# Weight buffers and branch outputs moved to other start addresses modulo 512 bytes, in a hybrid attention block

## The chip, the cores and the metric

The kernel runs on one core of a Trainium2 chip. The metric is device time in microseconds for one execution. Matmuls run on TensorE (PE in the profile, its weight loads PEld), elementwise work on VectorE (DVE), ScalarE (ACT) and GpSimd (POOL); SyncE (SP) issues most DMAs.

## What is computed

One layer of a hybrid decoder trunk, for a sequence of 256 rows of 2048 float32 values. Cut to what matters:

```python
proj = x @ w_in                       # 2048 -> 15632 columns, split into 14 parts
ya = gla(aq, ak, av, alr) * silu(agate)
yb = sliding_window(bq, bk, bv, sinks) * silu(bgate)
yc = moba(cq, ck, cv) * silu(cgate)   # 256 rows are one block: causal attention
up = einsum('bsnw,nwd->bsnd', stack([ya, yb, yc]), w_branch)
merged = sum(sigmoid(mgate + b_merge) * up, over the 3 branches)
out = merged @ w_o
return layer_norm(2 ** 0.25 * x + out)
```

Nearly all of the work is in the four groups of dense products: x with w_in, the three branch outputs with w_branch, and the merged stream with w_o.

## The kernel before, in words

**Precision.** Every float32 operand of a dense product is split into a high part (rounded to the format fp32r) and a low part (the rest, in fp32r too). A product is three fp32r matmuls: high with high, low with high, high with low.

**Weights.** `seq` lists all weight chunks in the order in which they are used. `emit_chunk` (line 112) handles one: SyncE loads it into a raw buffer (tag `wraw`, 4 buffers), ACT copies it to the high part (line 136, tag `whi`, 3 buffers), DVE subtracts to get the low part (line 137, tag `wlo`, 3 buffers). High and low buffers turn round together, so chunk i uses buffer i modulo 3 of both. `next_chunk` keeps two chunks ahead of the one in use. A chunk is 512 rows by 256 (or 260) columns, or 256 rows by 512 columns.

**Two forms of dense product.** In `mm3` (line 237) the weights are stationary and the activations move. For each block of 128 rows and each 128 columns there is a pair: line 242 has the high weights stationary and 512 moving columns (high and low part of the activation side by side), line 244 has the low weights stationary and 256 moving columns (the high part). `proj` calls it with `xhl` as moving operand, `up_mm` with a branch output (`ya`, `yb`, `yc`). There are 2080 such pairs, 384 of them with a branch output. In `nmm` (line 280) the activations are stationary and the weights move: lines 284, 285 and 286 have high, low and again high weights moving, 512, 260 or 256 columns at a time; the stationary operand is `xhl` or `mhl`, and that of line 284 is loaded again for line 285. There are 160 such triples of 512 columns (cv and the first three column groups of w_o), 128 of 260 columns (av), 32 of 256 columns (the fourth group of w_o, wo3 below) and 32 of 256 columns for the last group (wo4), whose weights lie in `wlasth` and `wlastl`, two buffers of the tag `y`.

**Order on TensorE.** While the dense products run, `tick` puts in steps of the attention jobs after each chunk; these are small matmuls between the pairs. Each matmul comes with a weight load of its own stationary operand, which the profile shows as PEld and which starts while the matmul before is running.

**Where the buffers begin.** Buffers are given out in the order of the pools, one behind another, each rounded up to 32 bytes; inside a pool, in the order of first use. Only the start modulo 512 bytes changes here. Before: all three low buffers begin at 160 and all three high buffers at 352, because 1152 columns are 4608 bytes, nine times 512, and the pool `stat` (3 times 64 bytes) stands between them. `xhl` and `mhl` (tag `x`) begin at 416, and so do both buffers of the tag `y`, which hold in turn `xst` (the raw x at the start), `ya`, `yb`, `yc`, `wlasth` and `wlastl`. A 128-column stationary operand is 512 bytes in a partition, and every step over rows or columns is a multiple of 512 bytes (except in av, whose rows are 260 columns), so each operand keeps its buffer's start modulo 512.

Of the kernel before, what the change touches and what calls it, by code (L numbers as in the profile page):

```python
# [9 lines left out]
F32 = mybir.dt.float32  # L10
F32R = mybir.dt.float32r
# [6 lines left out]
P = 128  # L18
S = 256
D = 2048  # L20
KT = D // P
# [7 lines left out]
NV = 260  # L29
KC = 4  # L30
RCOLS = KC * NV + 8
WCOLS = 1152
NWARM = 8


# [1 line left out]
def kernel(ctx: ExitStack, tc: tile.TileContext, xT: bass.AP, x: bass.AP, w_in: bass.AP,  # L37
                             w_up: bass.AP, gla_b: bass.AP, norm_g: bass.AP, sinks: bass.AP, b_merge: bass.AP,
                             w_branch: bass.AP, w_o: bass.AP, ln_g: bass.AP, ln_b: bass.AP, out: bass.AP):
    nc = tc.nc  # L40

    const = ctx.enter_context(tc.tile_pool(name="const", bufs=1))
    wraw = ctx.enter_context(tc.tile_pool(name="wraw", bufs=4))
    wlo = ctx.enter_context(tc.tile_pool(name="wlo", bufs=3))


    stat = ctx.enter_context(tc.tile_pool(name="stat", bufs=3))
    whi = ctx.enter_context(tc.tile_pool(name="whi", bufs=3))
    mvp = ctx.enter_context(tc.tile_pool(name="mvp", bufs=2))
    acts = ctx.enter_context(tc.tile_pool(name="acts", bufs=1))  # L50
    work = ctx.enter_context(tc.tile_pool(name="work", bufs=2))
    pp = ctx.enter_context(tc.tile_pool(name="pp", bufs=2, space=PSUM))
    pa = ctx.enter_context(tc.tile_pool(name="pa", bufs=4, space=PSUM))


    seq = []

    def deep(cols):
        return 2 if cols == 512 else KC

    def plan(src, rows, col0, cols, name):
        kc = deep(cols)
        for h in range(rows // (kc * P)):
            seq.append((src, h * kc * P, col0, cols, f"{name}_{h}"))
# [33 lines left out]
    for g, (c0, cols) in enumerate(OUT_COLS):  # L98
        plan(w_o, D, c0, cols, f"wo{g}")

    AHEAD = 2
    ready = []
    state = {"out": 0, "in": 0}
    last = {}

    def load_x(k0, k1):
        xs = xst[:, k0:k1, :]
        nc.sync.dma_start(xs, xT[:, k0:k1, :])
        nc.scalar.copy(xhl[:, k0:k1, 0:S], xs)
        nc.vector.tensor_tensor(xhl[:, k0:k1, S:2 * S], xs, xhl[:, k0:k1, 0:S].bitcast(F32), op=ALU.subtract)  # L110

    def emit_chunk():
        i = state["in"]
        state["in"] += 1
        src, row0, col0, cols, name = seq[i]
        kc = deep(cols)

        def shaped(t):
            return t.rearrange("p (k c) -> p k c", c=cols)
        raw = shaped(wraw.tile([P, RCOLS], F32, tag="wraw", name=f"w{name}")[:, :kc * cols])  # L120
        if name.startswith("wo4_"):
            if not last:
                last["h"] = acts.tile([P, KT, 256], F32R, tag="y", name="wlasth", bufs=2)
                last["l"] = acts.tile([P, KT, 256], F32R, tag="y", name="wlastl", bufs=2)
            k0 = KC * int(name[4:])
            hi, lo = last["h"][:, k0:k0 + KC, :], last["l"][:, k0:k0 + KC, :]
        else:
            hi = shaped(whi.tile([P, WCOLS], F32R, tag="whi", name=f"h{name}")[:, :kc * cols])
            lo = shaped(wlo.tile([P, WCOLS], F32R, tag="wlo", name=f"l{name}")[:, :kc * cols])
        view = src[row0:row0 + kc * P, col0:col0 + cols].rearrange("(k p) c -> p k c", p=P)  # L130
        cuts = [0, 1, 2] if i < 2 else [0, kc]
        for a, b in zip(cuts, cuts[1:]):
            if name.startswith("aq_"):
                load_x(row0 // P + a, row0 // P + b)
            nc.sync.dma_start(raw[:, a:b, :], view[:, a:b, :])
            nc.scalar.copy(hi[:, a:b, :], raw[:, a:b, :])  # L136
            nc.vector.tensor_tensor(lo[:, a:b, :], raw[:, a:b, :], hi[:, a:b, :].bitcast(F32), op=ALU.subtract)  # L137
        ready.append((name, hi, lo))

    def next_chunk(name):  # L140
        while state["in"] < len(seq) and state["in"] <= state["out"] + AHEAD:
            emit_chunk()
        got, hi, lo = ready[state["out"]]
        assert got == name, (got, name)
        state["out"] += 1
        return hi, lo
# [14 lines left out]
        while jobs:  # L161
            tick()

    xhl = acts.tile([P, KT, 2 * S], F32R, tag="x", name="xhl")
    xst = acts.tile([P, KT, S], F32, tag="y", name="xst", bufs=2)


    wz = const.tile([P, 512], mybir.dt.bfloat16, name="wz")
# [134 lines left out]
    def to_y(y, kt, o, gate, name):  # L303
        t = work.tile([P, S], F32, tag="q1", name=f"ty{name}", bufs=4)
        nc.vector.scalar_tensor_tensor(t, o, 0.5, gate, op0=ALU.mult, op1=ALU.mult)
        nc.scalar.copy(y[:, kt, 0:S], t)
        nc.gpsimd.tensor_tensor(y[:, kt, S:2 * S], t, y[:, kt, 0:S].bitcast(F32), op=ALU.subtract)
# [6 lines left out]
    for k in range(0, KT, 2):  # L314
        hi, lo = next_chunk(f"aq_{k // 2}")
# [8 lines left out]
        nc.scalar.copy(av[:, :, NV * g:NV * (g + 1)], ps[:, :, 0:NV])  # L324
    agate = act_tile("agate")

    ya = acts.tile([P, 8, 2 * S], F32R, tag="y", name="ya", bufs=2)
    aq = aqk[:, 0:4, :]
    ak = aqk[:, 4:8, :]
    IT = 1.0 / 16.0  # L330
# [168 lines left out]
    def front_job():  # L499
        yield from gla_job()  # L500
        while not done:
            yield 1
        yield from keys_job()
        yield from in_turn(swa_job, 8, 6)
# [31 lines left out]
                nc.scalar.copy(ks[rows, g, 0, :], src)  # L536
                nc.vector.tensor_tensor(ks[rows, g, 1, :], src, ks[rows, g, 0, :].bitcast(F32), op=ALU.subtract)

    yb = acts.tile([P, 8, 2 * S], F32R, tag="y", name="yb", bufs=2)

    def swa_job(hp):

# [10 lines left out]
        nc.gpsimd.dma_start(qs[0:64, 1, :], ql[64:128, :])  # L553
        yield from wait(4)
        sm = work.tile([P, 2, 2, P], F32, tag="sm", name=f"smb{hp}", bufs=2)
        st = stat.tile([P, 12], F32, tag="st", name=f"stb{hp}")
        nm, den, es = (st[:, 4 * i:4 * i + 4].rearrange("p (j t) -> p j t", j=2) for i in range(3))
        for j in range(2):
            ps = pa.tile([P, 4, P], F32, tag="pa", name=f"sb{hp}{j}")
# [120 lines left out]
    for g in range(4):  # L680
        gate_to(cgate[:, 2 * g:2 * g + 2, :], f"cg{g}")

    yc = acts.tile([P, 8, 2 * S], F32R, tag="y", name="yc", bufs=2)

    def moba_job(hp):
        scale = 128.0 ** -0.5
        sm = work.tile([P, 2, 3 * P], F32, tag="sm", name=f"smc{hp}", bufs=2)
        st = stat.tile([P, 12], F32, tag="st", name=f"stc{hp}")
        nm, den = (st[:, 4 * i:4 * i + 4].rearrange("p (t j) -> p t j", t=2) for i in range(2))
        for j in range(2):  # L690
            h = 2 * hp + j
            ps = pa.tile([P, 512], F32, tag="pa", name=f"sc{hp}{j}")
            nc.tensor.matmul(ps[:, 0:P], cq[:, h, 0:P], ck[:, h, 0:P], start=True, stop=True)
            nc.tensor.matmul(ps[:, P:3 * P], cq[:, h, P:S], ck[:, h, :], start=True, stop=True)
            nc.vector.scalar_tensor_tensor(sm[:, j, :], ps[:, 0:3 * P], scale,
                                           mska.rearrange("p a b -> p (a b)"), op0=ALU.mult, op1=ALU.add)
        parts = (slice(0, P), slice(P, 3 * P))
        for t in range(2):
            nc.vector.tensor_reduce(nm[:, t, :], sm[:, :, parts[t]], axis=AX.X, op=ALU.max, negate=True)
        for j in range(2):  # L700
            for t in range(2):
                nc.scalar.activation(sm[:, j, parts[t]], sm[:, j, parts[t]], AF.Exp, bias=nm[:, t, j:j + 1],
                                     accum_out=den[:, t, j:j + 1])
        nc.vector.reciprocal(den, den)
        for j in range(2):
            for t in range(2):
                nc.vector.tensor_scalar(sm[:, j, parts[t]], sm[:, j, parts[t]], den[:, t, j:j + 1], None,
                                        op0=ALU.mult)
        yield 1
        yield 1  # L710
        yield 1
        ptb = work.tile([P, 2, 3 * P], F32, tag="ptb", name=f"ptbc{hp}", bufs=1)
        for j in range(2):
            pt = pa.tile([P, 512], F32, tag="pa", name=f"ptc{hp}{j}")
            for b in range(3):
                nc.tensor.transpose(pt[:, b * P:(b + 1) * P], sm[:, j, b * P:(b + 1) * P], ident)
            nc.scalar.copy(ptb[:, j, :], pt[:, 0:3 * P])
        yield 1
        po = pa.tile([P, 2, S], F32, tag="pa", name=f"oc{hp}")
        for j in range(2):  # L720
            vs = slice((2 * hp + j) * P, (2 * hp + j + 1) * P)
            nc.tensor.matmul(po[:, j, :], cv[:, 0, vs], ptb[:, j, 0:S], start=True, stop=False,
                             skip_group_check=True)
            nc.tensor.matmul(po[:, j, P:S], cv[:, 1, vs], ptb[:, j, S:3 * P], start=False, stop=True,
                             skip_group_check=True)
        for j in range(2):
            h = 2 * hp + j
            to_y(yc, h, po[:, j, :], cgate[:, h, :], f"c{h}")

    jobs.append(in_turn(moba_job, 4, 4))  # L730
    merge(1, yb)
    drain()
    merge(2, yc)

    mhl = acts.tile([P, KT, 2 * S], F32R, tag="x", name="mhl")
    for dg in range(8):
        ks = slice(2 * dg, 2 * dg + 2)
        nc.scalar.activation(mhl[:, ks, 0:S], merged[dg], AF.Copy, scale=0.5)
# [90 lines left out]
```

## Time and profile before

| what | value |
|---|---|
| median of 3 runs | 965.49 us (964.96 to 965.79) |
| the profiled execution | 964.69 us |
| its span, first to last instruction | 963.0 us |
| PE busy | 946.2 us, 98% of the span, 5598 matmuls |
| PEld, DVE, ACT, POOL busy | 833.9, 633.7, 500.3, 93.0 us |
| mean granted TensorE clock | 0.995 |

Of the rows of the page and the trace: a matmul's duration covers its way through a pipeline, so durations of successive matmuls overlap; how fast they follow one another is read from their starts. In the timeline the columns are the start in us, the duration in us, the engine, the line, the operation, output and inputs by name, the shape and the count. In groups by line they are the line, engine, operation, names, shape and count, then the busy time in us of the group (overlaps counted once) and the mean duration in ns of one, then idle time before. Where a group's matmuls are longer than the distance from each to the next but one of another line, its busy time is that of the whole stage.

### The profile page before, as it was taken

What the parts mean: (1) busy time and instruction counts of PE and PEld (TensorE: products, weight loads), DVE (VectorE), ACT (ScalarE), POOL (GpSimd) and SP (SyncE); (2) the same over time, 40 slices, a digit from 0 to 9 for tenths busy, and PEclk for the clock granted to TensorE, in tenths of its full rate; (3) what the DMA queues carried; (4) which work ended last, traced back from release to release, by engine and by line L of the source; (5) the groups of instructions that cost most, each with busy time, mean ns of one, the idle gap of its engine ahead of it and who ended that gap; (6) DMA issues with size and microseconds to landing.
All of it is one profiled execution on the core that took longest, in us unless ns stands there. A gap on an engine that the chain in (4) does not pass through costs nothing.

```text
span 963.0 us, 14360 instructions
## 1 busy us (share of the span) xinstructions
PE 946.2 (98%) x5598; PEld 833.9 (87%) x5598; DVE 633.7 (66%) x780; ACT 500.3 (52%) x735; POOL 93.0 (10%) x127
## 2 busy tenths in 40 slices
PE   8999999999999999999999999999999999999995
PEld 6899889998888888888888888888888888888885
DVE  6544698758878888865544456665656565685556
ACT  6444564457566666644444445654545454564341
POOL 8000000003112322310000000110000000000003
PEclk9999999999999999999999999999999999999998
DMA  9766665555766666676766666487666666655652
GB/s 309 202 194 183 181 174 170 152 137 155 208 180 183 184 169 192 175 221 196 197 188 185 196 190 183 131 263 220 196 197 192 190 191 194 196 185 190 191 177 88
DMA packets 164052, 180.64 MB, mean 188 GB/s; under 512 B 6048, under 2 KB 150336, under 8 KB 163472
## 3 DMA queue, kind: packets, MB, share of 16 engines
q1 hardware_dynamic: 161552, 174.02, 62.5%
q0 software_dynamic: 2144, 5.51, 1.8%
q8 instruction: 44, 0.72, 0.3%
q10 hardware_dynamic: 288, 0.20, 0.1%
q14 instruction: 24, 0.20, 0.1%
HBM read 176.43 MB, written 2.10 MB: 185 GB/s over the span
## 4 chain that ended last, share of the span: by engine, by line
PE 93%; DVE 4%; DMA 1%; issue 1%; ACT 1%; SPq 0%; POOL 0%; DVEq 0%
PE psmg L242 18%; PE psmg L244 9%; PE pu L242 9%; PE pu L244 4%; PE psbq L242 3%; PE psag L242 3%; PE pscq L242 3%; PE pscg L242 3%; PE psck L242 3%; PE pswo L285 3%; PE pswo L284 3%; PE pswo L286 3%; PE psav L284 2%; PE psav L285 2%; PE psav L286 2%; PE pscv L285 2%
## 5 line engine op out<-in xcount | busy, mean ns | idle before, releaser
L242 PE MATMUL psmg<-xhl,hmg 128*128 128x512 f32 x768 | 264.6, 391 | 0.0
L244 PE MATMUL psmg<-xhl,lmg 128*128 128x256 f32 x768 | 212.1, 276 | 0.0
L137 DVE TENSOR_TENSOR lmg<-wmg,hmg 128x1024 fp32r<-128x1024 f32 x96 | 120.2, 1252 | 75.1 <-ACT hmg L136 75.1
L242 PEld LDWEIGHTS psmg<-xhl,hmg 128*128 128x128 f32 x768 | 144.2, 188 | 29.2
L136 ACT CAST hmg<-wmg 128x1024 fp32r<-128x1024 f32 x96 | 100.6, 1048 | 100.4 <-PE psmg L242 34.1
L244 PEld LDWEIGHTS psmg<-xhl,lmg 128*128 128x128 f32 x768 | 144.2, 188 | 0.1
L137 DVE TENSOR_TENSOR lwb<-wwb,hwb 128x1024 fp32r<-128x1024 f32 x48 | 58.8, 1225 | 38.7 <-ACT hwb L136 38.6
L136 ACT CAST hwb<-wwb 128x1024 fp32r<-128x1024 f32 x48 | 50.3, 1047 | 50.8 <-PE psmg L242 46.9
L137 DVE TENSOR_TENSOR lwo<-wwo,hwo 128x1024 fp32r<-128x1024 f32 x28 | 34.2, 1222 | 27.9 <-ACT hwo L136 27.9
L136 ACT CAST hwo<-wwo 128x1024 fp32r<-128x1024 f32 x28 | 29.4, 1050 | 42.0 <-PE pswo L286 38.9
L285 PE MATMUL pswo<-lwo,mhl 128*128 128x512 f32 (+1 forms) x128 | 47.3, 369 | 0.0
L284 PE MATMUL pswo<-hwo,mhl 128*128 128x512 f32 (+1 forms) x128 | 47.2, 368 | 0.0
L286 PE MATMUL pswo<-hwo,mhl 128*128 128x512 f32 (+1 forms) x128 | 46.6, 364 | 0.0
L242 PE MATMUL psbq<-xhl,hbq 128*128 128x512 f32 x128 | 45.6, 399 | 0.0
L242 PE MATMUL psbg<-xhl,hbg 128*128 128x512 f32 x128 | 44.7, 393 | 0.0
L242 PE MATMUL psag<-xhl,hag 128*128 128x512 f32 x128 | 44.6, 393 | 0.0
L242 PE MATMUL pu<-yb,hwb 128*128 128x512 f32 x128 | 44.2, 391 | 0.0
L242 PE MATMUL pu<-ya,hwb 128*128 128x512 f32 x128 | 44.2, 390 | 0.0
L242 PE MATMUL pu<-yc,hwb 128*128 128x512 f32 x128 | 43.9, 389 | 0.0
L242 PE MATMUL pscq<-xhl,hcq 128*128 128x512 f32 x128 | 43.6, 389 | 0.0
L242 PE MATMUL pscg<-xhl,hcg 128*128 128x512 f32 x128 | 43.6, 389 | 0.0
L242 PE MATMUL psck<-xhl,hck 128*128 128x512 f32 x128 | 43.6, 389 | 0.0
(309 smaller groups left out, 2343.7 us busy)
## 6 DMA issues: line engine op xcount, KB each, us to landing
wmg<-in_w_in_dram SPq DMA_DIRECT2D x96, 512.0 KB, 3.7
wwb<-in_w_branch_dram SPq DMA_DIRECT2D x48, 512.0 KB, 3.5
wwo<-in_w_o_dram SPq DMA_DIRECT2D x32, 512.0 KB, 4.6
wav<-in_w_in_dram SPq DMA_DIRECT2D x16, 520.0 KB, 3.7
wag<-in_w_in_dram SPq DMA_DIRECT2D x16, 512.0 KB, 3.9
wbq<-in_w_in_dram SPq DMA_DIRECT2D x16, 512.0 KB, 3.7
wbg<-in_w_in_dram SPq DMA_DIRECT2D x16, 512.0 KB, 3.7
wcq<-in_w_in_dram SPq DMA_DIRECT2D x16, 512.0 KB, 3.7
```

Of the source, the lines that this page charges most:

```text
L136: nc.scalar.copy(hi[:, a:b, :], raw[:, a:b, :])
L137: nc.vector.tensor_tensor(lo[:, a:b, :], raw[:, a:b, :], hi[:, a:b, :].bitcast(F32), op=ALU.subtract)
L242: nc.tensor.matmul(ps, hi[:, k, c], rhs[:, k0 + k, :], start=first and k == 0, stop=False, skip_group_check=True)
L244: nc.tensor.matmul(ps[:, 0:S], lo[:, k, c], rhs[:, k0 + k, 0:S], start=False, stop=last and k == kc - 1, skip_group_check=True)
L284: nc.tensor.matmul(ps[:, t, :cols], sh, hi[:, k, :], start=kk == 0, stop=False, skip_group_check=True)
L285: nc.tensor.matmul(ps[:, t, :cols], sh, lo[:, k, :], start=False, stop=False, skip_group_check=True)
L286: nc.tensor.matmul(ps[:, t, :cols], sl, hi[:, k, :], start=False, stop=kk == KT - 1, skip_group_check=True)
```

## The change

The widths of the high and low buffers differ and are no longer multiples of 512 bytes, so each of the three buffers begins elsewhere; two small pads (64 bytes each, written once by GpSimd) and the pool `mvp` (64 bytes) stand around them; the pool `stat` goes, and its tile becomes a tag of `work` with three buffers as before; the tiles of the tags `x` and `y` get 48 and 32 more columns. After it, modulo 512, the low buffers begin at 224, 288 and 352 (buffers 0, 1, 2), the high buffers at 480, 96 and 224; `xhl` and `mhl` stay at 416; the `y` buffers begin at 96 (`xst`, `yb`, `wlasth`) and 224 (`ya`, `yc`, `wlastl`). No instruction but the two memsets is added or removed, and no loop changes.

```diff
-WCOLS = 1152
+LCOLS = 1040
+HCOLS = 1056
...
+    pad0 = ctx.enter_context(tc.tile_pool(name="pad0", bufs=1))
     wlo = ctx.enter_context(tc.tile_pool(name="wlo", bufs=3))
-    stat = ctx.enter_context(tc.tile_pool(name="stat", bufs=3))
+    mvp = ctx.enter_context(tc.tile_pool(name="mvp", bufs=2))
     whi = ctx.enter_context(tc.tile_pool(name="whi", bufs=3))
-    mvp = ctx.enter_context(tc.tile_pool(name="mvp", bufs=2))
+    pad1 = ctx.enter_context(tc.tile_pool(name="pad1", bufs=1))
...
+    for pool in (pad0, pad1):
+        nc.gpsimd.memset(pool.tile([P, 16], F32, tag="pad", name=f"pad{pool is pad1:d}"), 0.0)
...
+    def y_tile(dt, name):
+        return acts.tile([P, KT * S + 32], dt, tag="y", name=name, bufs=2)[:, 0:KT * S]
...
-                last["h"] = acts.tile([P, KT, 256], F32R, tag="y", name="wlasth", bufs=2)
-                last["l"] = acts.tile([P, KT, 256], F32R, tag="y", name="wlastl", bufs=2)
+                last["h"] = y_tile(F32R, "wlasth").rearrange("p (k c) -> p k c", k=KT)
+                last["l"] = y_tile(F32R, "wlastl").rearrange("p (k c) -> p k c", k=KT)
...
-            hi = shaped(whi.tile([P, WCOLS], F32R, tag="whi", name=f"h{name}")[:, :kc * cols])
-            lo = shaped(wlo.tile([P, WCOLS], F32R, tag="wlo", name=f"l{name}")[:, :kc * cols])
+            hi = shaped(whi.tile([P, HCOLS], F32R, tag="whi", name=f"h{name}")[:, :kc * cols])
+            lo = shaped(wlo.tile([P, LCOLS], F32R, tag="wlo", name=f"l{name}")[:, :kc * cols])
...
-    xhl = acts.tile([P, KT, 2 * S], F32R, tag="x", name="xhl")
-    xst = acts.tile([P, KT, S], F32, tag="y", name="xst", bufs=2)
+    xhl = acts.tile([P, KT * 2 * S + 48], F32R, tag="x", name="xhl")[:, 0:KT * 2 * S].rearrange("p (k c) -> p k c", k=KT)
+    xst = y_tile(F32, "xst").rearrange("p (k c) -> p k c", k=KT)
...
-    ya = acts.tile([P, 8, 2 * S], F32R, tag="y", name="ya", bufs=2)
+    ya = y_tile(F32R, "ya").rearrange("p (k c) -> p k c", k=8)
...
-        st = stat.tile([P, 12], F32, tag="st", name=f"stb{hp}")
+        st = work.tile([P, 12], F32, tag="st", name=f"stb{hp}", bufs=3)
```

(`yb`, `yc`, `mhl` and the second `st` change in the same way as `ya`, `xhl` and the first `st`.)

## Rows read from the trace of the kernel before

**Rows 1.** The page: span, PE and PEld busy, and the chain by engine.

```profile
span 963.0 us, 14360 instructions
...
PE 946.2 (98%) x5598; PEld 833.9 (87%) x5598; DVE 633.7 (66%) x780; ACT 500.3 (52%) x735; POOL 93.0 (10%) x127
...
PE 93%; DVE 4%; DMA 1%; issue 1%; ACT 1%; SPq 0%; POOL 0%; DVEq 0%
```

**Rows 2.** Waits of PE: who it waited for, total us, times, longest.

```profile
PE psbg L244 <- DVE lbg L137: 1.5, 2, 1.3
```

**Rows 3.** Timeline of PE in ck: one pair and the next.

```profile
470.26 0.39 PE L242 MATMUL psck<-xhl,hck 128*128 128x512 f32 x1
470.49 0.28 PE L244 MATMUL psck<-xhl,lck 128*128 128x256 f32 x1
470.60 0.39 PE L242 MATMUL psck<-xhl,hck 128*128 128x512 f32 x1
```

**Rows 4.** Groups of PE by line and shape: the line 242 of four stages.

```profile
L242 PE MATMUL psmg<-xhl,hmg 128*128 128x512 f32 x768 | 264.6, 391 | 0.0
L242 PE MATMUL psbq<-xhl,hbq 128*128 128x512 f32 x128 | 45.6, 399 | 0.0
...
L242 PE MATMUL psag<-xhl,hag 128*128 128x512 f32 x128 | 44.6, 393 | 0.0
...
L242 PE MATMUL psck<-xhl,hck 128*128 128x512 f32 x128 | 43.6, 389 | 0.0
```

**Rows 5.** Timeline of PE in bq: a pair, and four pairs after its start.

```profile
177.98 0.40 PE L242 MATMUL psbq<-xhl,hbq 128*128 128x512 f32 x1
178.21 0.28 PE L244 MATMUL psbq<-xhl,lbq 128*128 128x256 f32 x1
...
179.38 0.40 PE L242 MATMUL psbq<-xhl,hbq 128*128 128x512 f32 x1
```

**Rows 6.** Timeline of PE in w_o, 512 columns: line 284, 13 triples apart.

```profile
900.15 0.40 PE L284 MATMUL pswo<-hwo,mhl 128*128 128x512 f32 x1
...
909.30 0.40 PE L284 MATMUL pswo<-hwo,mhl 128*128 128x512 f32 x1
```

**Rows 7.** Timeline of PE in av, 260 columns: line 284, 8 triples apart.

```profile
87.75 0.28 PE L284 MATMUL psav<-hav,xhl 128*128 128x260 f32 x1
...
90.62 0.28 PE L284 MATMUL psav<-hav,xhl 128*128 128x260 f32 x1
```

**Rows 8.** Timeline of PE in wo3, 256 columns: line 284, 11 triples apart.

```profile
932.17 0.28 PE L284 MATMUL pswo<-hwo,mhl 128*128 128x256 f32 x1
...
936.06 0.28 PE L284 MATMUL pswo<-hwo,mhl 128*128 128x256 f32 x1
```

**Rows 9.** Timeline of PE in wo4, weights in the y buffers: line 284, 14 triples apart.

```profile
940.66 0.28 PE L284 MATMUL pswo<-wlasth,mhl 128*128 128x256 f32 x1
...
945.69 0.28 PE L284 MATMUL pswo<-wlasth,mhl 128*128 128x256 f32 x1
```

**Rows 10.** Windows: length, busy us (count) of PE, PEld, DVE, ACT, POOL, clock, DMA share.

```profile
464.00:506.00 42.00, 42.00 (x235) 36.56 (x234) 21.62 (x20) 17.68 (x19) 0.00 (x0) 1.00 0.70 198
178.00:179.60 1.60, 1.60 (x11) 1.39 (x10) 1.46 (x2) 1.16 (x3) 0.00 (x0) 1.00 0.90 266
900.00:910.00 10.00, 10.00 (x45) 8.00 (x43) 6.19 (x8) 4.20 (x4) 0.00 (x0) 1.00 0.56 172
...
940.00:944.00 4.00, 4.00 (x35) 4.00 (x35) 2.10 (x5) 0.81 (x1) 0.00 (x0) 1.00 0.00 0
```

**Rows 11.** Timeline of PE and POOL: two attention matmuls, POOL's last set-up, its first user.

```profile
288.39 0.40 PE L596 MATMUL ob<-ph,vz 128*64 128x512 f32 x1
288.63 0.28 PE L598 MATMUL ob<-pl,vz 128*128 128x256 f32 x1
...
16.97 0.25 POOL L369 MEMSET alr<- 128x192 f32 x1
...
25.95 0.56 POOL L235 CAST lmask<-lmf 128x448 int32<-128x448 f32 x1
...
106.67 0.62 PE L354 MATMUL pdd<-hld,ones 128*128 128x512 f32 x2
```

More of the change, by code (lines that the diff above doesn't have):

```diff
@@ L537, in keys_job @@
                 nc.vector.tensor_tensor(ks[rows, g, 1, :], src, ks[rows, g, 0, :].bitcast(F32), op=ALU.subtract)
-    yb = acts.tile([P, 8, 2 * S], F32R, tag="y", name="yb", bufs=2)
+    yb = y_tile(F32R, "yb").rearrange("p (k c) -> p k c", k=8)
     def swa_job(hp):
@@ L681 @@
         gate_to(cgate[:, 2 * g:2 * g + 2, :], f"cg{g}")
-    yc = acts.tile([P, 8, 2 * S], F32R, tag="y", name="yc", bufs=2)
+    yc = y_tile(F32R, "yc").rearrange("p (k c) -> p k c", k=8)
     def moba_job(hp):
@@ L687, in moba_job @@
         sm = work.tile([P, 2, 3 * P], F32, tag="sm", name=f"smc{hp}", bufs=2)
-        st = stat.tile([P, 12], F32, tag="st", name=f"stc{hp}")
+        st = work.tile([P, 12], F32, tag="st", name=f"stc{hp}", bufs=3)
         nm, den = (st[:, 4 * i:4 * i + 4].rearrange("p (t j) -> p t j", t=2) for i in range(2))
@@ L733 @@
     merge(2, yc)
-    mhl = acts.tile([P, KT, 2 * S], F32R, tag="x", name="mhl")
+    mhl = acts.tile([P, KT * 2 * S + 48], F32R, tag="x", name="mhl")[:, 0:KT * 2 * S].rearrange("p (k c) -> p k c", k=KT)
     for dg in range(8):
```

## The prediction

> **What bounds the kernel now.** I read the page first: TensorE is busy for 98% of the span and the chain that ended last is 93% TensorE [rows 1]. The waits of TensorE come next, and there is almost nothing in them: past the start-up the longest total is 1.5 us, for a low part that DVE had not finished [rows 2]. So the time is the sum of the distances from each matmul's start to the next, and these I read from the timeline, stage by stage.
>
> In ck a pair (512 and 256 moving columns) takes 0.23 + 0.11 us [rows 3]; over the whole stage 43.6 us for 128 pairs, 340 ns a pair [rows 4], or 0.443 ns a column. In bq the same two instructions on the same addresses modulo 512 take 1.40 us for four pairs, 350 ns each [rows 5]. I counted the starts of line 242 that lie 0.35 us apart in the whole timeline: about 310 of the 2080 pairs, nearly all in ag, bq and the first pairs after attention matmuls; they cost 310 x 10 ns = 3.1 us. The busy times of bq and ag, 2.0 and 1.0 us above ck's [rows 4], agree with that, as they hold some restarts too.
>
> The projections with moving weights are slower for each column. 512 columns: 9.15 us for 13 triples, 703.8 ns each [rows 6], against 680 at ck's rate. 260 columns: 2.87 us for 8, 358.8 ns [rows 7], against 345.3. 256 columns: 3.89 us for 11, 353.6 ns [rows 8], against 340. And wo4, the same three instructions with the weights in the y buffers: 5.03 us for 14, 359.3 ns [rows 9].
>
> [...] What differs between wo3 and wo4 is where the operands begin. While a matmul streams its moving operand, the load for the next one reads its stationary operand; call the distance (start of the next stationary minus start of the moving operand) modulo 512. It is 256 at line 242 and 448 at line 244 (340 ns a pair, or 350); 64, 256, 64 in the triples; 0 in wo4. Nothing measured is faster than 0.443 ns a column, whatever the distance, so I take that as free of conflict.
>
> **The change, part by part.** *The new distances* (buffers 0, 1, 2 in turn, a third of the pairs each):
> - Pairs on x: line 242 320, 384, 448; line 244 64, 192, 320.
> - Pairs on ya and yc: line 242 0, 64, 128; line 244 256, 384, 0. On yb: 128, 192, 256 and 384, 0, 128.
> - Triples: high weights 448, 320, 192, low weights 192, 128, 64; wo4 320 and 192.
>
> *Pairs on x, 1696 of them.* Today's combination (256, 448) does not come back. Bounds: nothing (they hold 340), and the dearest rows, 234.6 ns for 512 columns [rows 6] and 119.8 for 256 [rows 9], so +14.4 a pair. No row shows these distances. The nearest row is bq, where the same instructions fell out of step and paid 10. I take half, 5 ns: the good step has to be found again with each chunk, since every chunk brings other distances. 1696 x 5 = 8.5 us, less the 3.1 paid already: +5.4 us.
>
> *Pairs on branch outputs, 384.* For ya and yc each of the three buffers has one distance of 0 or 64; a distance of 0 costs 359.3 / 3 - 113.3 = 6.4 ns at 256 columns [rows 9], and about 10 at 512 columns, where an attention matmul with both operands at one place modulo 512 takes 0.24 us [rows 11]. I take 6.7: 256 x 6.7 = 1.7 us. For yb one pair in three has the distance 0, the rest are priced as pairs on x: 0.7 us. Together +2.4 us, between 0 and 384 x 14.4 = 5.5.
>
> *Projections.* What they pay today is (703.8 - 680) x 160 = 3.8 us, (358.8 - 345.3) x 128 = 1.7, 13.6 x 32 = 0.4 and 19.3 x 32 = 0.6, in all 6.5 us [rows 6 to 9]. Of their distances 0 and 256 go altogether and 64 stays for one buffer of three at line 285. Bounds: all 6.5 saved, or none (the dearest price for each would add about 3). I take half: -3.3 us.
>
> *The rest.* Two memsets of 64 bytes a partition on GpSimd: a memset twelve times as large takes 0.25 us, and GpSimd is through with its set-up at 26.5 us while TensorE wants `ones` first at 106.7 [rows 11]; nothing. Without that cover it would be 0.5 us. The `st` tile keeps three buffers, the tags keep their counts, no queue gets a DMA more: no new wait. DVE's and ACT's conversions may get a little faster or slower; hidden as long as TensorE waits for them no more than today [rows 2]; if that cover went, the low parts of line 137 would be late first.
>
> **Sum.** 5.4 + 2.4 - 3.3 = +4.5 us. The profiled execution took 964.69 us (span 963.0 and 1.7 around it), 0.8 below the median of the runs shown; 964.69 + 4.5 + 0.8 = 970.0 us. A measurement of this kernel can tell about 0.2%, 2 us, from no change.
>
> [...] wo3 and wo4 differ by 5.7 ns a triple, with the same instructions and shapes [rows 8, 9]. [...]
>
> **Rivals.**
> 1. *Faster.* The pairs stay at 340 because distances from 64 up are all free, and only the projections and the 350s change. For it: ck holds 340 for 128 pairs without one slip [rows 4], and the zero of wo4, the dearest for 256 columns, is gone. Against it: wo3 pays with 64 and 256. Half of the projections' excess gives 965.5 - 3.3 = 962.2; all of it and the 350s, 965.5 - 9.6 = 955.9. Chance 0.33.
> 2. *No change.* The step of the pairs (340 or 350) comes from how a stage starts and not from places, and the projections' rates from their form. For it: bq and ck have the same places and differ [rows 4, 5]. Against it: wo3 and wo4. That the buffers would not lie where the change says is part of this case: 965.5. Chance 0.12.
> 3. *Much slower, and by one mechanism:* with other distances in each chunk of 8 pairs the pairs never fall into step, all run at 350 or worse. 2080 x 10 - 3.1 = +17.7, so 983.2; it decides once more than a quarter of the pairs on x stay at 350. At the dearest rows it would be 2080 x 14.4 - 3.1 = +26.9, so 992. Chance 0.13.
>
> **How the numbers follow.** My forecast, a mix that costs 2 to 11 us, has 0.42. Slower by over 0.2% is 0.42 + 0.13 = 0.55, faster 0.33, within 0.2% 0.12. The range reaches down to rival 1 at nearly its full saving (957) and up to rival 3 at 350 for all (985); beyond lie a perfect saving and the dearest rows. Both signs hold much of the chance; the forecast's own range is 967.5 to 976.
>
> **What would show it.** In the profile after: starts of line 242 in ck more than 0.34 us apart, in a rhythm of three chunks; ya's and yc's pairs slower than yb's; wo4 faster than 359 ns a triple; cv and w_o faster than 703.8. PE waits and clock as before. I am wrong if ck still takes 43.6 us for 128 pairs, or if the projections do not move.

## The result, and the profile after

The changed kernel takes **981.35 us** (median of 4 runs, 981.01 to 981.68) against 965.64 us for the kernel before (4 runs, 964.96 to 966.08): a ratio of 1.0163, 95% interval 1.0146 to 1.0181. I had forecast 970.0 us. The sign was right and the range held, but the size was 15.7 us where I had 4.5.

The page after, with the lines that answer to [rows 1] and [rows 4] (code lines are 7 higher: 249 and 251 are the pair, 291 to 293 the triple):

```profile
span 979.4 us, 14362 instructions
...
PE 963.8 (98%) x5598; PEld 845.4 (86%) x5598; DVE 633.6 (65%) x780; ACT 500.5 (51%) x735; POOL 93.2 (10%) x129
...
PE 93%; DVE 4%; issue 1%; DMA 1%; ACT 0%; POOL 0%; SPq 0%; DVEq 0%
...
L249 PE MATMUL psmg<-xhl,hmg 128*128 128x512 f32 x768 | 272.0, 396 | 0.0
...
L249 PE MATMUL psbq<-xhl,hbq 128*128 128x512 f32 x128 | 46.0, 400 | 0.0
...
L249 PE MATMUL psag<-xhl,hag 128*128 128x512 f32 x128 | 45.2, 395 | 0.0
...
L249 PE MATMUL psck<-xhl,hck 128*128 128x512 f32 x128 | 44.9, 394 | 0.0
```

The same 5598 matmuls keep TensorE busy for 17.6 us longer (963.8 against 946.2); DVE's busy time is where it was (633.6 against 633.7), ACT's too (500.5 against 500.3). No wait has come in: the one of [rows 2] stands with 1.0 us.

```profile
PE psbg L251 <- DVE lbg L144: 1.0, 1, 1.0
```

The clock is not it either. In the windows of ck, of 12 triples of w_o and of 17 triples of wo4 (columns as in [rows 10]) it is 1.00, as before, and in wo4 no DMA runs, before or after (share 0.00):

```profile
462.44:507.33 44.89, 44.89 (x258) 39.30 (x257) 22.02 (x20) 18.71 (x20) 0.00 (x0) 1.00 0.68 188
904.67:912.98 8.31, 8.31 (x37) 6.76 (x36) 3.68 (x4) 3.15 (x3) 0.00 (x0) 1.00 0.66 199
956.14:962.15 6.01, 6.01 (x53) 6.01 (x52) 2.36 (x6) 0.93 (x1) 0.00 (x0) 1.00 0.00 0
```

So only the distances between starts have changed. The timeline of PE after, in ck: the second pair of a chunk and the start of its eighth, for three chunks in turn (149 to 151 of `seq`, counted from 0), then w_o with 512 columns, 12 triples apart, then wo4, 17 triples apart:

```profile
465.62 0.39 PE L249 MATMUL psck<-xhl,hck 128*128 128x512 f32 x1
465.85 0.28 PE L251 MATMUL psck<-xhl,lck 128*128 128x256 f32 x1
...
467.70 0.39 PE L249 MATMUL psck<-xhl,hck 128*128 128x512 f32 x1
...
468.39 0.40 PE L249 MATMUL psck<-xhl,hck 128*128 128x512 f32 x1
468.62 0.28 PE L251 MATMUL psck<-xhl,lck 128*128 128x256 f32 x1
...
470.51 0.40 PE L249 MATMUL psck<-xhl,hck 128*128 128x512 f32 x1
...
471.20 0.40 PE L249 MATMUL psck<-xhl,hck 128*128 128x512 f32 x1
471.44 0.28 PE L251 MATMUL psck<-xhl,lck 128*128 128x256 f32 x1
...
473.32 0.40 PE L249 MATMUL psck<-xhl,hck 128*128 128x512 f32 x1
...
904.67 0.39 PE L291 MATMUL pswo<-hwo,mhl 128*128 128x512 f32 x1
...
912.98 0.39 PE L291 MATMUL pswo<-hwo,mhl 128*128 128x512 f32 x1
...
956.14 0.28 PE L291 MATMUL pswo<-wlasth,mhl 128*128 128x256 f32 x1
...
962.15 0.28 PE L291 MATMUL pswo<-wlasth,mhl 128*128 128x256 f32 x1
```

Six pairs take 2.08 us in the first of these chunks (346.7 ns a pair) and 2.12 us in the other two (353.3), where [rows 3] had 340. From the second pair on the step is steady in each. The 346.7 is the step that uni_b1, below, shows at buffer 1's places, and 353.3 that of buffer 2 (uni_b2). So the buffers do not come round as chunk i in buffer i modulo 3, by which chunk 149 would lie in buffer 2; in which of the other two buffers the next two chunks lie, their equal steps do not say. A triple of 512 columns is down to 8.31 / 12 = 692.5 ns (703.8 in [rows 6]), one of wo4 to 6.01 / 17 = 353.5 (359.3 in [rows 9]).

Summed over the whole trace, from each dense matmul's start to the next matmul's start on PE, in us:

| part | before | after | difference |
|---|---|---|---|
| pairs on x, aq | 25.17 | 26.78 | +1.61 |
| pairs on x, ak, ag, bq, bkv, bg | 168.79 | 170.76 | +1.97 |
| pairs on x, mg | 262.91 | 270.43 | +7.52 |
| pairs on x, cq, ck, cg | 130.59 | 134.67 | +4.08 |
| pairs on ya, yb, yc | 131.56 | 135.11 | +3.55 |
| av | 45.89 | 46.12 | +0.23 |
| cv, wo0 to wo2 | 112.52 | 110.74 | -1.78 |
| wo3, wo4 | 22.69 | 22.52 | -0.17 |

Of aq's 1.61 about 1.2 is not the change: four of the kernels below in which the pairs on x keep their distances (shift32, y_alone, best, kick) need 26.3 to 26.5 us there. The profiled execution of before was quicker in aq, but its first dense matmul also came later, at 5.55 us against 4.76 to 4.97 in those four. That leaves about 14.0 us for the pairs on x, 3.55 for those on branch outputs and -1.7 for the projections: about 15.8 us, against 15.7 in the medians. All other matmuls behind the first dense one sum to 45.3 us in both kernels.

### The profile page after: what moved, and what is told of

It reads as the page before. It is cut to its first block, busy times and chain, and to the rows that moved or that the text cites. A ratio compares the mean times of both kernels' runs of the same rounds, so it can differ in the third digit from the quotient of the medians.

```text
span 979.4 us, 14362 instructions
## 1 busy us (share of the span) xinstructions
PE 963.8 (98%) x5598; PEld 845.4 (86%) x5598; DVE 633.6 (65%) x780; ACT 500.5 (51%) x735; POOL 93.2 (10%) x129
## 4 chain that ended last, share of the span: by engine, by line
PE 93%; DVE 4%; issue 1%; DMA 1%; ACT 0%; POOL 0%; SPq 0%; DVEq 0%
PE psmg L249 18%; PE psmg L251 9%; PE pu L249 9%; PE pu L251 4%; PE psbq L249 3%; PE pscq L249 3%; PE pscg L249 3%; PE psck L249 3%; PE psag L249 3%; PE pswo L291 3%; PE pswo L293 3%; PE pswo L292 3%; PE psav L293 2%; PE psav L291 2%; PE psav L292 2%; PE psbq L251 2%
## 5 line engine op out<-in xcount | busy, mean ns | idle before, releaser
L249 PE MATMUL psmg<-xhl,hmg 128*128 128x512 f32 x768 | 272.0, 396 | 0.0
L251 PE MATMUL psmg<-xhl,lmg 128*128 128x256 f32 x768 | 215.6, 281 | 0.0
L249 PE MATMUL pscq<-xhl,hcq 128*128 128x512 f32 x128 | 44.9, 394 | 0.0
L249 PE MATMUL pscg<-xhl,hcg 128*128 128x512 f32 x128 | 44.9, 394 | 0.0
L249 PE MATMUL psck<-xhl,hck 128*128 128x512 f32 x128 | 44.9, 394 | 0.0
```

Source lines behind the costliest of these rows:

```text
L249: nc.tensor.matmul(ps, hi[:, k, c], rhs[:, k0 + k, :], start=first and k == 0, stop=False, skip_group_check=True)
L251: nc.tensor.matmul(ps[:, 0:S], lo[:, k, c], rhs[:, k0 + k, 0:S], start=False, stop=last and k == kc - 1, skip_group_check=True)
```

## The experiments

I write (a, b) for the two distances modulo 512. For a pair they are (start of the low weights minus start of the moving operand, start of the high weights minus the same); for a triple (start of the activations minus start of the high weights, start of the activations minus start of the low weights). Before, all pairs have (256, 448). Theory D: each combination has its own steady step. Theory R, mine from the prediction: the step is lost and has to be found again because the distances change with each chunk. Theory L: absolute places count (how a row of operands is cut at multiples of 64). Theory F: there are combinations faster than 340 ns.

### One buffer position for all chunks: uni_b1, uni_b2

Three pads put all low buffers at one place and all high buffers at one place, those of after's buffer 1 (288 and 96) and of its buffer 2 (352 and 224). Every chunk then has the same distances, (384, 192) in the one kernel and (448, 320) in the other; the branch outputs stay at 416.

```diff
+    pad0 = ctx.enter_context(tc.tile_pool(name="pad0", bufs=1))
     wlo = ctx.enter_context(tc.tile_pool(name="wlo", bufs=3))
...
+    pad1 = ctx.enter_context(tc.tile_pool(name="pad1", bufs=1))
     whi = ctx.enter_context(tc.tile_pool(name="whi", bufs=3))
...
+    pad2 = ctx.enter_context(tc.tile_pool(name="pad2", bufs=1))
     acts = ctx.enter_context(tc.tile_pool(name="acts", bufs=1))
...
```

> The kernel before, with all three low buffers at 288 and all three high buffers at 96 (those of buffer 1 in the changed kernel), x and y at 416 as before; distances 384 at line 242's and 192 at line 244's place, the same for every chunk. Theory D (each combination of distances has a step of its own): ck takes 44.4 us for 128 pairs, 346.7 ns a pair, as the chunks of buffer 1 do in the changed kernel; the run lands near 976 us. Theory R (what costs is that the distances change with every chunk, and a pair has to find its step again): ck stays at 43.5 us, 340 ns a pair, and the run at 965 or a little less.

> The kernel before, with all low buffers at 352 and all high buffers at 224 (those of buffer 2 in the changed kernel); distances 448 and 320 for every chunk. Theory D: ck 45.2 us for 128 pairs, 353.3 ns a pair; the run near 988 us. Theory R: ck 43.5 us, the run at 965 or a little less.

Measured: 974.28 and 985.71 us, one run each, the kernel before 967.71 beside them. That is one run too, and above all nine runs of it beside w_alone and best (964.67 to 967.30), so in what follows the stages say more than these totals. The groups of the pair's first line in uni_b1:

```profile
L248 PE MATMUL psmg<-xhl,hmg 128*128 128x512 f32 x768 | 269.4, 391 | 0.0
...
L248 PE MATMUL psck<-xhl,hck 128*128 128x512 f32 x128 | 44.4, 389 | 0.0
```

and in uni_b2:

```profile
L248 PE MATMUL psmg<-xhl,hmg 128*128 128x512 f32 x768 | 273.8, 398 | 0.0
...
L248 PE MATMUL psck<-xhl,hck 128*128 128x512 f32 x128 | 45.3, 397 | 0.0
```

ck holds 346.7 and 353.3 ns a pair for all of its 128 pairs (its sums of starts are 44.37 and 45.23 us), the very steps of the changed kernel's ck. Nothing changes from chunk to chunk here, so R falls, and D stands.

### The same distances, 32 bytes further on: shift32

One pad of 32 bytes ahead of the low buffers moves low, high, x and y together, from odd to even multiples of 32. All distances stay.

```diff
+    pad0 = ctx.enter_context(tc.tile_pool(name="pad0", bufs=1))
     wlo = ctx.enter_context(tc.tile_pool(name="wlo", bufs=3))
...
```

> The kernel before with low and high buffers, x, y and all that lies behind them 32 bytes further: low 192, high 384, x and y 448, so that all of them begin at multiples of 64 and every distance is as before. Theory D in its plain form (only distances count): 340 ns a pair, 703 ns a 512-column triple, 965 us. Rival L (operands are read in pieces of 64 bytes, and an operand that begins in the middle of a piece reads one more of them, 17 for 16): pairs fall to between 320 and 326 ns, ck to between 41.0 and 41.8 us, the run to about 935 us.

Measured: 967.55 us, before 967.71.

```profile
L244 PE MATMUL psmg<-xhl,hmg 128*128 128x512 f32 x768 | 264.6, 391 | 0.0
...
L244 PE MATMUL psck<-xhl,hck 128*128 128x512 f32 x128 | 44.8, 395 | 0.0
```

mg is as in [rows 4], w_o's 512 columns take 67.51 us in both kernels. Nothing comes near L's 41.0 to 41.8 us for ck, so L falls, and mg and w_o keep their steps 32 bytes further on: there the distances count and not the places. But cq and ck went to 350 ns a pair, 1.3 us each, with the same distances at which they had held 340: an observation that I come back to with the last run.

### The branch outputs alone: y_alone

Only the tags `x` and `y` have after's widths; the weights stay at 160 and 352. (The 384 pairs on branch outputs then have (64, 256), for yb, or (448, 128), for ya and yc, and wo4 the distances 320 and 192.)

```diff
...
-    ya = acts.tile([P, 8, 2 * S], F32R, tag="y", name="ya", bufs=2)
+    ya = y_tile(F32R, "ya").rearrange("p (k c) -> p k c", k=8)
...
```

> The kernel before with the y buffers alone moved, to 96 and 224 as in the changed kernel; weights at 160 and 352. Pairs on x keep 340 ns under both theories. Pairs on ya and yc have the distances 448 and 128, those on yb 64 and 256, the same in every chunk. Theory R: 340 ns for them too (43.5 us for 128 pairs). Theory D: at least one of the two stages leaves 340, to a step 6.7 or 13.3 ns longer, so 44.4 or 45.2 us. wo4 (distances 320 and 192 in place of 0) falls from 360 to about 353 ns a triple under D. The run within 3 us of 966 us.

Measured: 968.28 us, before 967.71; the pairs on x stay at 340 in ck.

```profile
L245 PE MATMUL pu<-ya,hwb 128*128 128x512 f32 x128 | 45.6, 397 | 0.0
L245 PE MATMUL pu<-yb,hwb 128*128 128x512 f32 x128 | 45.0, 394 | 0.0
...
L245 PE MATMUL pu<-yc,hwb 128*128 128x512 f32 x128 | 44.7, 392 | 0.0
L245 PE MATMUL psck<-xhl,hck 128*128 128x512 f32 x128 | 43.6, 389 | 0.0
```

By their starts ya, yb, yc take 1.31, 0.85 and 0.89 us more than before, wo3 and wo4 together 0.19 less. ya and yc have one combination and yet two steps, 353.3 and 346.7 ns, and ya itself goes over to 346.7 in its last two chunks.

### The weights alone: w_alone

After without the wider tags, so that the branch outputs lie at 416 again.

```diff
-        return acts.tile([P, KT * S + 32], dt, tag="y", name=name, bufs=2)[:, 0:KT * S]
+        return acts.tile([P, KT * S], dt, tag="y", name=name, bufs=2)[:, 0:KT * S]
...
```

> The weights alone: high and low buffers as after, the branch outputs back at 416. If each combination of distances has its own step (the theory): the 1696 pairs on x cost what they cost after (+15 us), the 384 pairs on branch outputs now have the same distances as the pairs on x (351 ns a pair, +4.1 us against before), cv, av, wo0 to wo3 save 1.6 us and wo4 stays at 360 ns a triple: 965.6 + 15 + 4.1 - 1.6 = 983 us, slower than after although less is moved; ya, yb and yc take 44.9 us each. If the parts simply add up (each moved buffer costs something by itself): after's 981.3 less the 2.4 that the branch outputs cost when moved alone, 979 us, and ya, yb, yc at 43.8.

Measured: 981.51 us (4 runs, 981.29 to 982.02), ratio to before 1.0162 (1.0148 to 1.0176): as slow as after, within the measurement.

```profile
L249 PE MATMUL pu<-yc,hwb 128*128 128x512 f32 x128 | 45.4, 396 | 0.0
L249 PE MATMUL pu<-ya,hwb 128*128 128x512 f32 x128 | 45.3, 395 | 0.0
...
L249 PE MATMUL psck<-xhl,hck 128*128 128x512 f32 x128 | 44.9, 394 | 0.0
```

The stages are where D put them (by starts ya 45.19, yb 45.36, yc 45.08 us for an expected 44.9, or 43.8 if the parts added); the total came out between the two expectations, 983 and 979, mainly because the sum that I had written down for the first counted aq's 1.2 us as part of the change. What decides is the branch outputs: moved alone they cost 3.05 us in their own pairs, and taken back out of the change they gave nothing back, so the parts do not add. A pair pays by its combination, whichever operand was moved.

### Maps of the combinations: sweep64, sweep32

High and low tiles 128 columns wider, and each group of weights sliced at its own multiple of 64 bytes, so that the pairs meet all 64 combinations of multiples of 64; sweep32 does the same for odd multiples of 32.

```diff
-WCOLS = 1152
+WCOLS = 1152 + 128
...
-            hi = shaped(whi.tile([P, WCOLS], F32R, tag="whi", name=f"h{name}")[:, :kc * cols])
-            lo = shaped(wlo.tile([P, WCOLS], F32R, tag="wlo", name=f"l{name}")[:, :kc * cols])
+            a, b = (16 * v + 0 for v in place[name])
+            hi = shaped(whi.tile([P, WCOLS], F32R, tag="whi", name=f"h{name}")[:, a:a + kc * cols])
+            lo = shaped(wlo.tile([P, WCOLS], F32R, tag="wlo", name=f"l{name}")[:, b:b + kc * cols])
```

> The kernel before with high and low buffers 512 bytes wider, each weight group (a chunk, in av, cv and w_o) lying at its own multiple of 64 bytes inside them: one run goes through all 64 combinations of distances for the pairs, and most for the triples. [...] Rival F: 340 is only the best of the few combinations seen so far, and some groups settle at 320 to 333. The run between 965 and 985 us.

> The same with the high and low buffers 32 bytes further, so that all distances to x and y are odd multiples of 32. Theory D: the same steps, none below 340; Rival F: some groups between 320 and 333. If pieces of 64 bytes are what meets, a distance between two of the first run costs what the dearer of its neighbours costs or lies between them; the run between 965 and 990 us.

Measured: 978.61 and 979.87 us, before 965.98. The mg stage of sweep64 is spread over its combinations:

```profile
L257 PE MATMUL psmg<-xhl,hmg 128*128 128x512 f32 x768 | 271.1, 396 | 0.0
```

Its timeline at two combinations that differ in the high weights alone, (256, 192) in cq and (256, 0) in cg, six pairs apart each:

```profile
418.74 0.39 PE L257 MATMUL pscq<-xhl,hcq 128*128 128x512 f32 x1
...
420.78 0.39 PE L257 MATMUL pscq<-xhl,hcq 128*128 128x512 f32 x1
...
552.48 0.40 PE L257 MATMUL pscg<-xhl,hcg 128*128 128x512 f32 x1
...
554.60 0.40 PE L257 MATMUL pscg<-xhl,hcg 128*128 128x512 f32 x1
```

They are 2.04 / 6 = 340 and 2.12 / 6 = 353.3 ns a pair. Settled steps of a pair in these and the other kernels, read from the starts, ns:

| combinations | step |
|---|---|
| (256, 64), (256, 192), (256, 320), (256, 448), (0, 192), (0, 448) | 340 (at (256, 448) also 350) |
| (256, 0), (256, 128), (256, 384) | 352 to 353.3, in rhythms of three or five pairs |
| (256, 256) | 346.7 |
| all others in multiples of 64 | 346 to 355 |
| odd multiples of 32: (32, 96), (32, 352), (288, 96), (288, 352) | 343.3, as 342 and 345 in turn |
| all others in odd multiples of 32 | 346 to 355 |

None is below 340, and F falls. Of 64 combinations in multiples of 64 only six hold 340. The guess about pieces of 64 bytes fell too: (32, 96) and (32, 352) hold 343.3, less than any of their four neighbours in the first map (346.7 to 353.3). And D in its strict form, one step for each combination, does not hold everywhere: of the groups that met one combination twice some differ, at (0, 64) with 353.3 ns in ag and 350 in a branch product, and at (32, 96) ag goes over from 343.3 to about 352. For triples of 512 columns the spread is 680 to 707 ns: a chunk at (256, 0) had 680; (448, 192), (320, 128) and (192, 64), those of after, have 686.5, 693 and 691 (the last two in uni_b1 and uni_b2), and before's (64, 256), with 703.3, is among the dearest.

### A version from the maps: best

Before, with the pairs left at (256, 448) and only the moving weights of the projections put elsewhere within wider tiles: 512 columns at (256, 0), wo3 and wo4 at (64, 64), av from (384, 0).

```diff
+    def place(name):
+        if name.startswith("av"):
+            return (48, 64)
+        if name.startswith("wo3"):
+            return (0, 48)
+        if name.startswith(("cv", "wo")):
+            return (80, 64)
+        return 0, 0
...
+            a, b = place(name)
+            hi = shaped(whi.tile([P, WCOLS], F32R, tag="whi", name=f"h{name}")[:, a:a + kc * cols])
+            lo = shaped(wlo.tile([P, WCOLS], F32R, tag="wlo", name=f"l{name}")[:, b:b + kc * cols])
...
```

> Before, with only the operands of the projections moved to the distances that the maps showed as cheapest: 512 columns at (256, 0), 256 columns (wo3 and wo4) at (64, 64), 260 columns from (384, 0); all pairs stay at (256, 448). The theory: 160 triples of 512 columns fall from 703 to about 681 ns (-3.6 us), 32 of wo3 from 353.6 to 340 (-0.4), 32 of wo4 from 359.5 to 340 (-0.6), av from 2867 to 2845 ns a chunk of 24 matmuls (-0.35): 965.6 - 5.0 = 960.7 us, 0.5% faster. The rival, that the 680 ns of one chunk was a chance of its neighbours and not of its distances: cv and w_o at 690 or more, 963.5 us or above.

Measured: **961.65 us** (5 runs, 961.22 to 963.89) against 965.77 (9 runs, 964.67 to 967.30), ratio 0.9962, interval 0.9949 to 0.9976: faster than both kernels. Its timeline in w_o, 13 triples of 512 columns apart, then wo3, then wo4, 14 triples apart each:

```profile
899.74 0.39 PE L297 MATMUL pswo<-hwo,mhl 128*128 128x512 f32 x1
...
908.58 0.39 PE L297 MATMUL pswo<-hwo,mhl 128*128 128x512 f32 x1
...
925.96 0.28 PE L297 MATMUL pswo<-hwo,mhl 128*128 128x256 f32 x1
...
930.90 0.28 PE L297 MATMUL pswo<-hwo,mhl 128*128 128x256 f32 x1
...
936.20 0.28 PE L297 MATMUL pswo<-wlasth,mhl 128*128 128x256 f32 x1
...
941.15 0.28 PE L297 MATMUL pswo<-wlasth,mhl 128*128 128x256 f32 x1
```

8.84 / 13 = 680 ns: from the third triple of cv and of w_o on every one holds it, and cv and wo0 to wo2 together fall from 112.52 to 108.86 us, 3.66 for an expected 3.6. The rest failed: wo3 stays at 4.94 / 14 = 352.9 ns, though one chunk in the map had 340 at the same (64, 64); wo4 gains 6 ns a triple instead of 19; av holds 2867 ns a chunk instead of 2845. For wo3 and av a step seen in one chunk was not a property of the combination alone.

### What stood before: kick

To see where a second step at the same places comes from, one more matmul, of 16 to 486 columns in steps of 10, goes ahead of each of the 48 chunks of cq, ck and cg. Nothing uses its result; no place changes.

```diff
             hi, lo = next_chunk(f"{name}_{h}")
+            if name[:2] in ("cq", "ck", "cg"):
+                n = 16 + 10 * state.setdefault("kick", 0)
+                state["kick"] += 1
+                kick = pa.tile([P, 512], F32, tag="pa", name=f"kick{name}{h}")
+                nc.tensor.matmul(kick[:, 0:n], wz[:, 0:P], wz[:, 0:n], start=True, stop=True)
```

> Before, with one more matmul, of 16 to 486 columns in steps of 10, ahead of each of the 48 chunks of cq, ck and cg (its result is used by nothing); all places stay, all pairs at (256, 448), and no attention matmul stands in these stages. [...] Theory of the second step (a stage has more than one steady rhythm at the same places, and what stood before it decides which): after some lengths all eight pairs of the chunk keep 340 ns, after others all eight keep another step such as 350; with half of the chunks at 350 another 1.9 us, 973 us. The rival (the rhythm belongs to the places, and 350 in bq comes from what other engines do beside the attention work): every one of the 48 chunks settles at 340, 971 us.

Measured: 973.43 us, before 964.75. The timeline of PE in cq: the chunk after 46 added columns, and the chunk after 56:

```profile
419.46 0.20 PE L259 MATMUL kickcq<-wz 128*128 128x46 bf16 x1
...
419.93 0.40 PE L242 MATMUL pscq<-xhl,hcq 128*128 128x512 f32 x1
...
422.03 0.40 PE L242 MATMUL pscq<-xhl,hcq 128*128 128x512 f32 x1
...
422.38 0.20 PE L259 MATMUL kickcq<-wz 128*128 128x56 bf16 x1
...
423.56 0.39 PE L242 MATMUL pscq<-xhl,hcq 128*128 128x512 f32 x1
...
424.92 0.39 PE L242 MATMUL pscq<-xhl,hcq 128*128 128x512 f32 x1
```

After 46 columns six pairs take 2.10 us, 350 ns each, from the second pair to the last of the chunk; after 56 columns four pairs take 1.36, 340 each. Of the 48 chunks 10 kept 350 to their end (after 26, 46, 66, 296, 316, 376, 386, 416, 456 and 466 columns), 38 settled at 340 within four pairs. So (256, 448) has two steady rhythms, and what stood before the chunk picks one. The 350 of bq [rows 5], which begins with chunks that follow an attention matmul, and that of shift32's ck are the same two rhythms at the same distances; that ya and yc of y_alone differ, and that ya changes over, fits too, though at their combination it was not tried. 10 x 8 x 10 ns are 0.8 us, less than the 1.9 that I had put down for half of the chunks; most of the 8.7 us are the added matmuls themselves and the longer first pair after each (422.43 to 422.87 us after 56 columns, 0.44 us for 0.34). The 971 and 973 us expected hold 5.0 us for the added columns, a term that no run shows; in cq, after 56, 76 and 86 columns, a chunk that settles at 340 takes 2.87 to 2.88 us from its added matmul to the next one, 0.15 to 0.16 more than eight pairs at 340.

## Why the prediction missed

*What bounds the kernel* was right: the time is the sum of the distances between starts. No wait came in (1.0 us past the start-up), the clock is 1.00 in the three windows before and after, and traffic is not it: wo4 went from 359.3 to 353.5 ns a triple with no DMA in either kernel. In these runs the distances between the operands' starts modulo 512 bytes set the step, or the few steps of which a stage falls into one: ck has 340 ns a pair before, 346.7 in uni_b1 and 353.3 in uni_b2, and y_alone and the maps agree. So places matter: the same instructions at other addresses take 15.7 us longer.

*Pairs on x: the step that failed.* I took "half, 5 ns: the good step has to be found again with each chunk", in all +5.4 us. Measured, about +14.0. The reason was wrong and with it the size. In ck nothing is searched for: each chunk falls into its step with the second pair, but that step is 346.7 or 353.3 ns, 350.7 in the mean of ck, 10.7 ns above 340. With one position for all chunks (uni_b1) it is just as steady and just as long. The upper bound, +14.4 a pair, held. Bq's 10 ns without the half would have given 1696 x 10 - 3.1 = +13.9 us, but that would have been luck: bq's 350 is the second rhythm of the old distances (kick), not a price of the new ones. The 3.1 us itself came from a count that was too high: in the trace of before some 200 pairs, not 310, lie within 1 ns of 350; with the others between 340 and 355 they cost 2.8 us, so this moved the sum by little. The rows of before already told which end was nearer: of the five kinds of dense work that its trace held (the pairs and those of [rows 6 to 9]) only the pairs reached 0.443 ns a column, and I treated theirs as the rule, to be left for a moment, instead of as the exception.

*Pairs on branch outputs.* +3.55 us for +2.4; the bounds held. The price that I put on distances of 0 and 64 did not show: ya and yc, which have them, take 45.19 and 44.67 us, yb 45.25. The sign that I had named, ya and yc slower than yb, did not come. Distance 0 is not dear in itself: (0, 192) and (0, 448) hold 340. The combination counts, and my price for a single distance was the wrong kind of term.

*Projections.* -1.7 us for -3.3. The 512 columns went from 703 to 692 ns, 1.8 us less, about the half of their 3.8 that I had taken; av did not save at all (+0.23), wo3 and wo4 0.17 instead of a half of 1.0.

*The rest.* Two memsets, the `st` tile, the queues: nothing, as said; PE's waits are as short as before.

*The rivals.* Rival 3 had nearly the right time, 983.2: all pairs at 350 gives +17.7, the pairs measured +17.5, and the projections gave 1.7 back. Its mechanism, pairs that never fall into step, is not what happens. Rival 1 (all free from 64 up) fell with ck's 351. Rival 2 fell as a forecast, but a piece of it holds: kick shows that how a stage starts does choose between 340 and 350 at the same places. It is the smaller effect: in the kernel before it moves some 200 pairs by 10 ns, and the change moves nearly all 2080.

**What stays open.** Whether it is the weight load that meets the stream of the moving operand, as I had pictured it, is not shown: the runs vary where the operands begin, and loads run while matmuls do whatever the places (5588 of the 5598 loads before and 5591 after start during a matmul). Why no pair settled below 340, how what stands before picks the rhythm, and whether another matmul ahead of wo3, wo4 and av would bring them to the step that the map promised, no run here tells.

## What to carry to other kernels

When TensorE is never waited for and still slower per column in some stages than in others, compare the starts of successive matmuls, stage by stage, with the operands' start addresses modulo 512; here that was worth 1.6% between two layouts that differ otherwise only in two small memsets and the place of one small tile, and 0.4% more beyond the better of the two. A buffer's place is part of the kernel: a pool put in, or a tile made wider for other reasons, can move it. When a trace shows one combination that is quick and several that are slow, price a new one at the slow ones; here only 6 of 64 were as quick.

## What I had not expected of the hardware

- Many steps lie on a grid: 340, 346.7 and 353.3 ns a pair are 51, 52 and 53 times 6.67 ns, by which they differ, and 343.3 and 350 lie half-way between two of them.
- No combination of places gave a settled step below 340 ns a pair, in multiples of 64 or in odd multiples of 32.
- One layout has more than one steady rhythm: at (256, 448) a matmul of 46 columns ahead leaves a chunk at 350 ns to its end, one of 56 columns at 340.
- A distance is neither good nor bad alone: 256 on the first line of the pair gives 340 with 64, 192, 320 or 448 on the second, and 352 to 353.3 with 0, 128 or 384.
